# Cache attention of a sample group: four fp32 tiles of 32 columns side by side in place of high and low halves on the whole array

## The chip, the core and the metric

The kernel runs on one core of one Trainium2 chip. Its engines work from queues of their own: PE (TensorE: matmuls and transpositions), DVE (VectorE), ACT (ScalarE), POOL (GpSimd) and SP (SyncE, which here issues most DMAs). Matmul results go to PSUM, all else is held in SBUF. The metric is the device time of the core in microseconds, less is better.

## The reference, cut to what matters

One layer of a hybrid decoder in fp32, for two groups that share the weights: a prompt of 1024 tokens, and a sample group of 8 samples with 8 new tokens each (64 rows in all). The change touches the sample group's attention over its cache. Each sample has 1024 past tokens in 8 pages of 128, found through a page table; 4 heads, each with two maps of 64 (queries and keys) and values of 128:

```python
def diff_attn_block(qb, qpos_b, k, v, k_pos, rel_bias, lam):
    s = jnp.einsum('bqhcd,bkhcd->bchqk', qb, k) * (DIFF_HEAD_DIM ** -0.5)
    rel = qpos_b[:, None] - k_pos[None, :]
    bias = jnp.transpose(rel_bias[rel_bucket(rel)], (2, 0, 1))
    s = jnp.where(rel[None, None, None] >= 0, s + bias[None, None], NEG_INF)
    p = jax.nn.softmax(s, axis=-1)
    a = p[:, 0] - lam * p[:, 1]
    return jnp.einsum('bhqk,bkhe->bqhe', a, v)

k_past = cache_k[l][page_table].reshape(DB, past, N_DIFF_HEADS, 2 * DIFF_HEAD_DIM)
v_past = cache_v[l][page_table].reshape(DB, past, N_DIFF_HEADS, DIFF_V_DIM)
```

So there are 64 pages of K and 64 of V, 256 KB each. Around it: the input projection with three gate logits of width 1024, attention of the prompt, an attention over a memory, pooling, an output projection and a convolutional feed-forward block.

## The kernel before

**Number format.** Most matmuls have their operands split: `split` (L108 to 110) copies a fp32 tile, rounded, to a high half in the type fp32r (ACT, L109) and subtracts that from the tile for a low half (DVE or POOL, L110). A product is then three fp32r matmuls (high by high, high by low, low by high), each a single pass. A matmul with plain fp32 operands has two records in the trace.

**Gate logits.** Weights come in tiles `raw` (L159, two buffers, 512 KB each), are split into `hl` (five buffers; low half on POOL for these), and go to L178 (`mm_t`, prompt: `nat<-act,hl`, 24 matmuls of 512 columns for each result) and L195 (`mm_s`, sample rows: `nat<-hl,hs`). A result is copied out by `ev` (L831) and written to DRAM by `gl` (L832). There are 1344 of these L178 matmuls; nothing but the end of the layer's first half needs them, so they can fill TensorE wherever it would wait.

**What sets the order.** The program is written in stages, and when it is built a scheduler with a list of priorities puts the instructions of all stages into one fixed queue for each engine. That is how gate matmuls come to stand between those of cache attention. On the chip each queue runs strictly in order: an instruction whose operand is late holds up all behind it.

**Cache attention** (L553 to 699). Setting up: the queries are transposed, split and laid into `QS` with zeros around; the scores of the new keys against the new queries go through DRAM (`nk_d`) into `NKD`; the bias of the last 128 past positions is `dbt`. Then for each sample, twice four pages:
- `load_page` reads the page's number into a register of SP (L610) and issues the DMA (L611). The pages of K (`kr`) and V (`vr`) share three buffers of two pages each. A chain of order (`issue_after`) keeps the register read of a page behind the DMA of six pages earlier.
- The four pages are transposed head by head (L106, four transpositions of 128x128 into PSUM tiles `tp` or `av`), split into `kt`, and multiplied with `QS` by L631: 128 columns hold the high and low halves of the queries of both maps, all heads accumulate in one PSUM tile `big`.
- L651 and L652 add the halves into `E`, two samples above each other. For a pair of samples L656 subtracts the bias, L658 takes the maximum, L660 the exponential with its sum; `R` (L665) holds the reciprocal sums and the factor lambda, and L671 multiplies `E` with it in nine plain fp32 matmuls, which transposes and normalises the weights at once. They are split into `aTd`.
- The pair's V pages are split into `vh` and multiplied by L685, with 64 columns: high and low half of the weights of one sample. L688 does the new rows. The mask `hm1` keeps each head's own columns, and L695 sums the rows into `oS`.

After cache attention comes the prompt's attention (L706 to 777): per head the DMAs of `kn`, `vn`, `qT`, transpositions, scores (L741), softmax, values (L771), with gate matmuls between.

## Time and profile before

| | us |
|---|---|
| runs | 1871.69, 1870.64, 1865.92 |
| median of the runs | 1870.64 |
| profiled execution, span | 1869.5 |
| L178, the gate logits of the prompt, busy | 366.0 |
| L178, other projections, busy | 494.8 |
| L195, gate logits of the sample rows, busy | 86.4 |

The span runs from the first to the last record of the execution that was profiled. Busy times of matmuls overlap, since a matmul is counted from its start to the modelled end of its flow through the array while the next one has begun; the spacing of their starts is the price of one. The stages can be told by their first instructions: cache attention begins with the first transposition of a `kr` tile (358.5 us into the span), the prompt's attention with the first of a `kn` tile (606.7), and the projections of the two groups follow.

A row of a view of groups has the line, the engine, the operation, output and inputs by their names in the program, the shapes and the count; behind the bar the busy time in us and the mean of one in ns; behind a second bar the idle time ahead and what ended it. A row of the timeline has the start, the duration, the engine, the line and what runs. A row of the windows has the stretch and its length, the busy time of PE, PEld (weight loads), DVE, ACT and POOL in it, then that of SP, the mean granted clock of TensorE (1.00 is full), the busy share of the DMA engines and GB/s; an engine without work there may be missing.

### The profile page before, as it was taken

The page shows a single profiled execution, that of the slowest core. Times are in us where ns is not written, and L with a number is a line of the kernel's source. Part 1 is how long each engine was busy: PE and PEld are TensorE (multiplying, and loading weights), DVE is VectorE, ACT ScalarE, POOL GpSimd, SP SyncE. Part 2 cuts the span into 40 slices and gives each one's busy share as a digit, 9 for nine tenths or more (in the row PEclk, how much of TensorE's full clock was granted, in tenths as well). Part 3 has the DMA queues.
Part 4 walks back from the last instruction along what each step waited for, and adds up shares of the span by engine and source line. Part 5 has one row for each costly group of instructions (what it writes and reads, how often), then busy time and mean ns, then how long its engine had stood idle before and what let it go on. Part 6 is the DMA issues. An engine that isn't in the chain of part 4 may idle for free.

```text
span 1869.5 us, 22444 instructions
## 1 busy us (share of the span) xinstructions
PE 1807.6 (97%) x8329; PEld 1417.9 (76%) x8329; DVE 884.6 (47%) x1565; ACT 637.2 (34%) x1227; POOL 219.0 (12%) x263
## 2 busy tenths in 40 slices
PE   7999989999999999999999999999999999999997
PEld 5777866766666877777778788888888888888886
DVE  6411134255544667646733634353453453553547
ACT  5331235245444666634512432122122122221222
POOL 1113140212002342301210000000000000000000
PEclk9999999999999999999999999999999999999999
DMA  7341251365657332245561110120110110210202
GB/s 255 133 143 48 80 171 46 109 211 163 190 164 219 89 118 80 83 143 172 175 170 46 57 46 28 41 68 24 45 47 28 63 46 23 68 46 24 68 12 96
DMA packets 119457, 179.67 MB, mean 96 GB/s; under 512 B 23999, under 2 KB 61437, under 8 KB 119349
## 3 DMA queue, kind: packets, MB, share of 16 engines
q1 hardware_dynamic: 108821, 148.13, 25.9%
q0 software_dynamic: 10528, 30.12, 4.4%
q8 instruction: 65, 1.06, 0.2%
q14 instruction: 43, 0.35, 0.1%
HBM read 143.72 MB, written 34.55 MB: 95 GB/s over the span
## 4 chain that ended last, share of the span: by engine, by line
PE 78%; issue 8%; DVE 5%; DMA 4%; ACT 3%; POOL 1%; SPq 0%; POOLq 0%; ACTq 0%; DVEq 0%
PE big L178 30%; PE big L993 12%; PE nat L178 11%; PE nat L187 8%; PE nat L195 5%; PE tp L106 3%; PE av L771 2%; PE big L741 2%; DMA raw<-in_w_in 1%; PE big L631 1%; PE av L106 1%; PE big L685 1%; ACT hl L109 1%; PE av L542 1%; DMA kr<-in_cache_k 1%
## 5 line engine op out<-in xcount | busy, mean ns | idle before, releaser
L178 PE MATMUL big<-h,hl 128*128 128x512 f32 x2112 | 494.8, 394 | 0.0
L178 PEld LDWEIGHTS big<-h,hl 128*128 128x128 f32 x2112 | 395.1, 188 | 90.6 <-ACT h L109 0.3
L178 PE MATMUL nat<-act,hl 128*128 128x512 f32 x1344 | 366.0, 403 | 0.3 <-ACT ev L831 0.3
L178 PEld LDWEIGHTS nat<-act,hl 128*128 128x128 f32 x1344 | 243.7, 189 | 45.1 <-issue 2.3
L993 PE MATMUL big<-hl,ft 128*128 128x512 f32 x1056 | 241.5, 389 | 0.5 <-DVE x L995 0.5
L993 PEld LDWEIGHTS big<-hl,ft 128*128 128x128 f32 x1056 | 198.1, 188 | 42.3 <-DVE x L995 1.0
L109 ACT CAST hl<-raw 128x1024 fp32r<-128x1024 f32 x126 | 132.0, 1051 | 278.9 <-PE big L993 151.2
L110 DVE TENSOR_TENSOR hl<-raw,hl 128x1024 fp32r<-128x1024 f32 x102 | 124.4, 1222 | 162.4 <-ACT hl L109 160.7
L187 PE MATMUL nat<-hl,act 128*128 128x512 f32 x768 | 184.9, 399 | 5.9 <-DVE x1s L884 4.1
L187 PEld LDWEIGHTS nat<-hl,act 128*128 128x128 f32 x768 | 146.5, 192 | 38.1 <-issue 4.5
L995 DVE TENSOR_TENSOR x<-x,big 128x1024 f32<-128x1024 f32 x88 | 107.3, 1219 | 67.4 <-PE big L993 67.0
L958 POOL DMA_DIRECT2D out<-gu x22 | 11.9, 541 | 827.2 <-DVE gu L203 827.0
L922 DVE SCALAR_TENSOR_TENSOR t<-big,cwb,t 128x1023 f32<-128x1023 f32 x22 | 28.2, 1283 | 166.8 <-ACT t L921 166.8
L195 PE MATMUL nat<-hl,hs 128*128 128x512 f32 x336 | 86.4, 400 | 3.7 <-POOL hl L110 2.5
L195 PEld LDWEIGHTS nat<-hl,hs 128*128 128x128 f32 x336 | 63.1, 191 | 18.5 <-POOL hl L110 3.6
L949 DVE TENSOR_TENSOR t<-t,big 128x1024 f32<-128x1024 f32 x22 | 26.9, 1221 | 79.8 <-PE big L178 79.8
L110 POOL TENSOR_TENSOR hl<-raw,hl 128x1024 fp32r<-128x1024 f32 x24 | 58.3, 2434 | 43.6 <-ACT hl L109 40.3
L109 ACT CAST ft<-t 128x1024 fp32r<-128x1024 f32 x22 | 23.1, 1050 | 107.3 <-DVE t L949 107.3
L942 ACT COPY gc<-big 128x2 f32<-128x2 f32 x22 | 3.5, 160 | 162.0 <-PE big L178 162.0
L832 POOL DMA_DIRECT2D gl<-ev x48 | 26.3, 547 | 276.2 <-ACT ev L831 254.2
L110 DVE TENSOR_TENSOR vh<-vr,vh 128x512 fp32r<-128x512 f32 x64 | 46.6, 762 | 23.9 <-ACT vh L109 23.9
L752 ACT ACTIVATE E<-big,nm 128x128 f32<-128x128 f32 (+7 forms) x64 | 47.5, 742 | 22.5 <-DVE nm L749 11.7
(365 smaller groups left out, 2204.5 us busy)
## 6 DMA issues: line engine op xcount, KB each, us to landing
raw<-in_w_in SPq DMA_DIRECT2D x40, 512.0 KB
kr<-in_cache_k SPq DMA_DIRECT2D x64, 256.0 KB
vr<-in_cache_v SPq DMA_DIRECT2D x64, 256.0 KB
gl<-ev POOLq DMA_DIRECT2D x48, 256.0 KB, 2.8
raw<-in_w_ffn_gate SPq DMA_DIRECT2D x44, 256.0 KB
raw<-in_w_ffn_up SPq DMA_DIRECT2D x44, 256.0 KB
raw<-in_w_ffn_down SPq DMA_DIRECT2D x22, 512.0 KB
g<-gl SPq DMA_DIRECT2D x38, 256.0 KB
```

The lines of the kernel that those rows point to most:

```text
L106: nc.tensor.transpose(out, in_, ident[:n, :n])
L109: nc.scalar.copy(hi, src)
L110: (lo_eng or nc.vector).tensor_tensor(lo, src, hi.bitcast(F32), op=ALU.subtract)
L178: nc.tensor.matmul(out, wf(k, pw)[:, n0:n0 + P], acts[c][ph][:, k, :], start=(k == ks[0] and (pw, ph) == (0, 0)), stop=(k == ks[-1] and (p ...
L187: nc.tensor.matmul(out, acts[c][ph][:, k, o:o + P], wf(k, pw), start=(k == ks[0] and (pw, ph) == (0, 0)), stop=(k == ks[-1] and (pw, ph) = ...
L195: nc.tensor.matmul(out, stack[:, k, :], wf(k, pw), start=(k == ks[0] and pw == 0), stop=(k == ks[-1] and pw == 1))
L741: nc.tensor.matmul(S[:, k0:k0 + n], Qd[:, m, part, qs], Kst[:, m, k0:k0 + n], start=(part == 0), stop=(part == 1))
L752: nc.scalar.activation(E[:, :nk], S[:, :nk], AF.Exp, bias=nm, scale=-1.0, accum_out=ss[:, m:m + 1])
L771: nc.tensor.matmul(av[:, :P], aT[:, k * P:(k + 1) * P], vn[:, k0 + k], start=(k0 + k == 0), stop=(k0 + k == i))
L922: nc.vector.scalar_tensor_tensor(out[:, 1:], g[:, 0:T - 1], cwb[:, f, 1:2], out[:, 1:], op0=ALU.mult, op1=ALU.add)
L993: nc.tensor.matmul(pb_[:, nb], fts[k][:, ph, t * P:(t + 1) * P], wfs[nb](k, pw), start=(k == 0 and (pw, ph) == (0, 0)), stop=(k == 1 and ( ...
L995: nc.vector.tensor_tensor(x1[t], x1[t], pb_.rearrange("p c t -> p (c t)"), op=ALU.add)
```

## The change

Cache attention is laid out anew, with plain fp32 operands throughout:

- **Scores.** `QS` holds for each sample and head 32 columns of plain queries (two samples of a pair, two maps, eight rows; those of the other sample are zero). The transposed pages are copied whole into `kt`, even heads on ACT (L638), odd heads on DVE (L636). When all four heads are there, L644 runs four matmuls, one for each head, each with 32 columns of weights on its own quarter of the array's columns (`tile_position`), written one behind the other. Both samples of a pair accumulate in the same PSUM rows.
- **Weights.** `E` has the rows by head, sample, map, and 1152 columns; L652 and L653 copy the scores from PSUM on ACT, L654 subtracts the bias while copying the last 128 columns. The mask between samples for the new rows lies in `NKD`, which is filled with -1e30 and gets eight small DMAs instead of two. L667 and L670 form the transposed weights as before, but `aT` stays plain, with four buffers.
- **Values.** They are done for four samples at once, after the weights of two pairs: for each page number `kb`, L696 runs four matmuls side by side, one for each sample, on the pages of V as they are; the ninth group is the new rows (`vsf`). `hm1` and the selection matmul (now L704) run once for four samples.
- **Buffers.** The pages of K and V share five tiles of two pages instead of three.

```diff
-        qsT = dc.tile([P, 2, NH, TS], F32R, name="qsT")
+        QS = dc.tile([P, DB, NH, 32], F32, name="QS")
+        nc.gpsimd.memset(QS, 0.0)
...
-        nc.gpsimd.dma_start(bass.AP(nk_d.tensor, nk_d.offset, [[TS, TS], [8 * 512, 2 * NH], [1, TS]]),
-                            nks.rearrange("p (c t) -> p c t", t=TS))
-        NKD = dc.tile([P, DB // 2, DS], F32, name="NKD")
-        for par in range(2):
-            nc.gpsimd.dma_start(NKD[par * TS:par * TS + TS],
...
+        for c in range(2):
+            nc.gpsimd.dma_start(bass.AP(nk_d.tensor, nk_d.offset + c * 4096, [[TS, TS], [8192, NH], [1, TS]]),
+                                nks[:, c * 256:(c + 1) * 256].rearrange("p (h t) -> p h t", t=TS))
+        NKD = dc.tile([P, DB // 2, 2, DS], F32, name="NKD")
+        nc.gpsimd.memset(NKD, -1e30)
+        for h in range(NH):
+            for s2 in range(2):
+                r0 = h * 32 + s2 * 16
+                nc.gpsimd.dma_start(NKD[r0:r0 + 16, :, s2],
...
-        for b in range(DB):
...
-                    k_ = dc.tile([P, 2, 512], F32, tag="kr", bufs=3, name=f"kr{uid()}")
...
+        def scores(b, ch, Sb):
+            kr = []
+            for i in range(2):
+                k_ = dc.tile([P, 2, 512], F32, tag="kr", bufs=5, name=f"kr{uid()}")
+                for u in range(2):
+                    load_page(k_[:, u], cache_k, b * NPG + ch * 4 + i * 2 + u)
+                kr.append(k_)
+            kt = dc.tile([P, NH, 512], F32, tag="kt", bufs=2, name=f"kt{uid()}")
+            for h in range(NH):
+                pt = tpb()
+                for i in range(4):
+                    tr(pt[:, i * P:(i + 1) * P], kr[i // 2][:, i % 2, h * P:(h + 1) * P])
+                if h % 2:
+                    nc.vector.tensor_copy(kt[:, h], pt)
+                else:
+                    nc.scalar.copy(kt[:, h], pt)
+            first = None
+            for h in range(NH - 1, -1, -1):
+                with ExitStack() as es:
+                    if first is not None:
+                        es.enter_context(tc.issue_after(first.ins))
+                    m = nc.tensor.matmul(Sb[h * 32:(h + 1) * 32, ch], QS[:, b, h], kt[:, h], start=(b % 2 == 0),
+                                         stop=(b % 2 == 1), tile_position=(0, h * 32))
+                first = first or m
+
+        def weights(p, Sb):
+            E = dc.tile([P, 1152], F32, tag="E", bufs=2, name=f"Ed{p}")
+            nc.gpsimd.memset(E[:, 1024:1152], -1e30)
+            nc.vector.tensor_copy(E[:, 1024 + 16 * p:1040 + 16 * p], NKD[:, p].rearrange("p s t -> p (s t)"))
+            nc.scalar.copy(E[:, 0:512], Sb[:, 0])
+            nc.scalar.copy(E[:, 512:896], Sb[:, 1, 0:384])
+            nc.vector.tensor_tensor(E[:, 896:1024], Sb[:, 1, 384:512], dbt, op=ALU.subtract)
...
+            aT = dc.tile([P, 9, TS], F32, tag="aT", bufs=4, name=f"aTd{p}")
...
+            for kb in range(8):
+                nc.tensor.matmul(pa[:, kb * TS:(kb + 1) * TS], E[:, kb * P:(kb + 1) * P], R, start=True, stop=True)
+            nc.scalar.copy(aT[:, 0:8].rearrange("p k r -> p (k r)"), pa)
...
+        for g in range(2):
+            aTs = []
+            for p in (2 * g, 2 * g + 1):
+                Sb = big()
+                for b in (2 * p, 2 * p + 1):
+                    for ch in range(2):
+                        scores(b, ch, Sb)
+                aTs.append(weights(p, Sb))
+            X = big()[:, 0]
             for kb in range(9):
...
+                        vr = dc.tile([P, 2, 512], F32, tag="kr", bufs=5, name=f"vr{uid()}")
+                        for u in range(2):
+                            load_page(vr[:, u], cache_v, (4 * g + 2 * i + u) * NPG + kb)
...
+                        m = nc.tensor.matmul(X[bl * 32:(bl + 1) * 32],
+                                             aTs[bl // 2][:, kb, (bl % 2) * 32:(bl % 2) * 32 + 32],
+                                             vrs[bl // 2][:, bl % 2] if kb < 8 else vsf,
+                                             start=(kb == 0), stop=(kb == 8), tile_position=(0, bl * 32))
...
+            nc.vector.tensor_tensor(om, X, hm1, op=ALU.mult)
             pn = tpb()
...
+            nc.tensor.matmul(pn[:32], selb, om, start=True, stop=True)
+            nc.vector.tensor_copy(oS[g * 32:(g + 1) * 32], pn[:32])
```

The scheduler orders the queues anew. Three places are shown; a row there is the line, the operation, output and inputs with the numbers of their buffers, the shape of the output, and how many in a row.

**TensorE, the end of the first pair's scores.** Before, gate matmuls (L178, on the weights `hl`) stand ahead of the matmuls L671 that form the weights `tp` out of `Ed` and `R`, and behind them:

```order
L178 MATMUL nat_7266<-act_145,hl_7180 128x512 x2
L178 MATMUL nat_7266<-act_146,hl_7180 128x512
L178 MATMUL nat_7266<-act_145,hl_7180 128x512
L178 MATMUL nat_7266<-act_145,hl_7185 128x512
L178 MATMUL nat_7266<-act_146,hl_7185 128x512
L178 MATMUL nat_7266<-act_145,hl_7185 128x512
L671 MATMUL tp_2853<-R_2851,Ed_2666 128x64 x8
L671 MATMUL big_2854<-R_2851,Ed_2666 64x64
L178 MATMUL nat_7266<-act_145,hl_7185 128x512
```

Now, the transpositions of the last pages, the score group L644, the weights and the next sample's transpositions follow each other:

```order
L106 MATMUL av_2781<-ident,kr_2720 128x128 x2
L106 MATMUL av_2781<-ident,kr_2741 128x128 x2
L644 MATMUL big_2506<-kt_2762,QS 32x512 x4
L667 MATMUL tp_2807<-R_2804,Ed_2791 128x64 x8
L670 MATMUL av_2817<-R_2804,Ed_2791 128x64
L106 MATMUL av_2870<-ident,kr_2821 128x128
L106 MATMUL tp_2864<-ident,kr_2821 128x128 x2
```

The 27 gate matmuls that stood between the scores and the weights of the pair are no longer there.

**TensorE, the last values of the stage.** Before, the value matmuls (L685, on the split pages `vh`) alternate with gate matmuls:

```order
L685 MATMUL big_4744<-vh_4942,aTd_4754 64x512
L178 MATMUL nat_7770<-act_147,hl_7707 128x512
L685 MATMUL big_4744<-vh_4942,aTd_4754 64x512
L178 MATMUL nat_7770<-act_147,hl_7712 128x512
L685 MATMUL big_4744<-vh_4968,aTd_4754 64x512
L178 MATMUL nat_7770<-act_148,hl_7712 128x512
```

Now the value groups of samples 4 to 7 (L696) stand alone, and the next gate matmuls come behind them, on weights `hl` that are loaded later:

```order
L696 MATMUL big_4140<-vr_4484,aTd_4126 32x512 x2
L696 MATMUL big_4140<-vr_4463,aTd_3812 32x512 x2
L696 MATMUL big_4140<-vsf,aTd_4126 32x512 x2
L696 MATMUL big_4140<-vsf,aTd_3812 32x512 x2
L195 MATMUL nat_6955<-hl_6937,hs 128x512 x4
L704 MATMUL av_4515<-omd_4513,selb 32x512
L195 MATMUL nat_6955<-hl_6942,hs 128x512 x4
```

Counted over the whole stage (from the first transposition of `kr` to the first of `kn`), 453 matmuls of L178 and 36 of L195 stood in it before, 199 and 20 do now; the other 270 stand further back.

**SP, the end of the pages.** Before, the last page of V (L611) is followed by the DMAs of the prompt's attention, `NB` and `kn`; the weights of the gates (`raw`, L159) stood further ahead, twelve of them among the pages:

```order
L610 TENSOR_LOAD pgt
L610 ISA x2
L611 ISA
L611 DMA vr_4978<-in_cache_v 128x512
L706 DMA NB<-nb_d 128x256 x4
L710 DMA kn_5027<-k_d 128x8x128
```

Now four of the gates' weight tiles stand behind the last page, ahead of `NB` and `kn`, and one among the pages:

```order
L621 DMA vr_4484<-in_cache_v 128x512
L159 DMA raw_6935<-in_w_in 128x2x512
L159 DMA raw_6940<-in_w_in 128x2x512
L159 DMA raw_6945<-in_w_in 128x2x512
L159 DMA raw_6950<-in_w_in 128x2x512
L712 DMA NB<-nb_d 128x256 x4
L716 DMA kn_4528<-k_d 128x8x128
```

So the matmul L195 that follows the last value group works on the first of these tiles.

More of the change, by code (lines that the diff above doesn't have):

```diff
@@ L690, in hybrid_step @@
-            om = dc.tile([P, 512], F32, tag="om", bufs=2, name=f"omd{b}")
-            for bb in range(2):
-                nc.vector.tensor_tensor(om[bb * TS:(bb + 1) * TS], X[:TS, bb], hm1[:TS], op=ALU.mult)
-            pn = tpb()
-            o0 = 48 - 8 * (b - 1)
-            nc.tensor.matmul(pn[:TS], selb[:, o0:o0 + TS], om, start=True, stop=True)
-            if b == 1:
-                nc.vector.tensor_copy(oS, pn[:TS])
-            else:
-                nc.vector.tensor_tensor(oS, oS, pn[:TS], op=ALU.add)
+            for kb in range(8):
+                nc.tensor.matmul(pa[:, kb * TS:(kb + 1) * TS], E[:, kb * P:(kb + 1) * P], R, start=True, stop=True)
@@ new lines, in weights @@
+            nc.scalar.copy(aT[:, 0:8].rearrange("p k r -> p (k r)"), pa)
+            pn = tpb()
+            nc.tensor.matmul(pn[:, :TS], E[:, 1024:1152], R, start=True, stop=True)
+            nc.vector.tensor_copy(aT[:, 8], pn[:, :TS])
+            return aT
+        for g in range(2):
[7 more added lines that the diff above has]
+            X = big()[:, 0]
+            for kb in range(9):
+                vrs = []
+                if kb < 8:
+                    for i in range(2):
+                        vr = dc.tile([P, 2, 512], F32, tag="kr", bufs=5, name=f"vr{uid()}")
+                        for u in range(2):
+                            load_page(vr[:, u], cache_v, (4 * g + 2 * i + u) * NPG + kb)
+                        vrs.append(vr)
+                first = None
+                for bl in range(3, -1, -1):
+                    with ExitStack() as es:
+                        if first is not None:
+                            es.enter_context(tc.issue_after(first.ins))
+                        m = nc.tensor.matmul(X[bl * 32:(bl + 1) * 32],
+                                             aTs[bl // 2][:, kb, (bl % 2) * 32:(bl % 2) * 32 + 32],
+                                             vrs[bl // 2][:, bl % 2] if kb < 8 else vsf,
+                                             start=(kb == 0), stop=(kb == 8), tile_position=(0, bl * 32))
+                    first = first or m
+            om = dc.tile([P, 512], F32, tag="om", bufs=2, name=f"omd{g}")
+            nc.vector.tensor_tensor(om, X, hm1, op=ALU.mult)
+            pn = tpb()
+            nc.tensor.matmul(pn[:32], selb, om, start=True, stop=True)
+            nc.vector.tensor_copy(oS[g * 32:(g + 1) * 32], pn[:32])
```

119 lines of the change are left out of this document (31 added, 88 removed).

## The prediction

> **What bounds the kernel now.** I read the page from the top: the span, the engines' shares, the slices, then the chain that ended last.
>
> ```profile
> span 1869.5 us, 22444 instructions
> PE 1807.6 (97%) x8329; PEld 1417.9 (76%) x8329; DVE 884.6 (47%) x1565; ACT 637.2 (34%) x1227; POOL 219.0 (12%) x263
> PEclk9999999999999999999999999999999999999999
> PE 78%; issue 8%; DVE 5%; DMA 4%; ACT 3%; POOL 1%; SPq 0%; POOLq 0%; ACTq 0%; DVEq 0%
> ```
>
> TensorE is busy for 97% of the span, at full clock. So a microsecond of matmul taken out counts, as long as something else is ready to run in its place. Next come the stages: the windows from the first transposition of a K page (358.5) to the first of the prompt's keys (606.7), and the two stages after it.
>
> ```profile
> 358.50:606.70 248.20, 236.47 (x1098) 163.07 (x1097) 124.47 (x207) 111.37 (x184) 35.55 (x33) 0.99 0.59 184
> 606.70:786.00 179.30, 173.23 (x991) 139.24 (x990) 117.97 (x305) 117.97 (x309) 60.79 (x68) 1.00 0.28 85
> 786.00:860.00 74.00, 69.94 (x319) 53.42 (x318) 40.19 (x130) 33.54 (x70) 9.41 (x12) 1.00 0.52 167
> ```
>
> The cache stage takes 248.2 us, PE busy 236.5. What keeps it busy is told by the groups of that window, the largest of which is not cache attention at all but gate logits put between:
>
> ```profile
> L178 PE MATMUL nat<-act,hl 128*128 128x512 f32 x454 | 132.4, 404 | 0.0
> L631 PE MATMUL big<-kt,QS 128*128 128x512 f32 x128 | 51.6, 447 | 3.5 <-ACT kt L109 2.5 <-DVE kt L110 0.9
> L685 PE MATMUL big<-vh,aTd 128*64 128x512 f32 x128 | 44.0, 413 | 4.2 <-DVE vh L110 4.1
> L106 PE MATMUL tp<-ident,kr 128*128 128x128 f32 x128 | 26.9, 278 | 3.6 <-DMA kr<-in_cache_k 3.6
> L106 PE MATMUL av<-ident,kr 128*128 128x128 f32 x128 | 23.7, 273 | 0.0
> L195 PE MATMUL nat<-hl,hs 128*128 128x512 f32 x36 | 11.2, 430 | 0.0
> L695 PE MATMUL av<-omd,selb 128*64 128x512 f32 x8 | 4.3, 618 | 0.0
> ```
>
> These busy times overlap, so I price a matmul by its spacing in a dense run, from the timeline:
>
> ```profile
> 512.26 6.28 PE L178 MATMUL nat<-act,hl 128*128 128x512 f32 x27
> 371.26 0.60 PE L106 MATMUL tp<-ident,kr 128*128 128x128 f32 x4
> 518.87 1.97 PE L671 MATMUL tp<-R,Ed 128*128 128x64 f32 x16 [0.33 <-DVE R L665]
> 276.39 1.09 PE L508 MATMUL big<-mv,PTs 128*32 128x256 f32 x16
> 277.41 0.66 PE L106 MATMUL tp<-ident,mk 128*128 128x128 f32 x4
> ```
>
> ```profile
> 302.81 0.86 PE big L523 x2
> ```
>
> A split matmul of 512 columns is 6.28/27 = 0.23 us. A transposition is (0.60 - 0.27)/3 = 0.11, 0.44 for four. L671 has 16 records for 8 matmuls of the program: plain fp32 is two passes, about 2.0 us for a pair's nine. **The best row for the change is L508**: plain fp32 on 32 columns, four tiles, in the attention over the memory. Sixteen records of 256 columns last from 276.39 until the next start at 277.41, 1.02 us. On the whole array two plain passes of 512 columns (L523, from the chain in order of time) take 0.86, so sixteen passes of 256 one after another would take 3.4. Four tiles do run side by side here, each four passes of 256 deep; the changed kernel issues two passes of 512 deep in each: **1.02 us for a group of four**.
>
> **What goes and what comes, on PE.** Before: 453 + 36 gate matmuls x 0.23 = 112.5; 256 transpositions 27.9; L671 8.0; 256 score and value matmuls of L631 and L685, and 16 of the new rows' values, x 0.23 = 62.6; L695, eight passes of 512 at half speed, 3.5. Sum 214.5 of 248.2, so the stage holds **33.7 us of waiting**; much of it hides in busy time (L631 and L685 are busy 95.6 us for 256 x 0.23 = 58.9). After: 16 score groups and 18 value groups x 1.02 = 34.7; L704 has half of L695's passes, 1.7; transpositions and weights stay, 35.9. That is 72.3 against 102.0: **29.7 us less PE work**. DVE and ACT lose the splits of K and V; DVE is busy for 124 of 248 us, so this saves nothing by itself.
>
> But the order shows the second effect. The changed stage holds only 199 + 20 gate matmuls: **270 are moved behind it, 270 x 0.23 = 62.1 us**, into the stages after, which the windows above show already full (173 of 179, 70 of 74). The stage must get shorter by more than 62.1 us before anything is won. Its PE work is now 219 x 0.23 + 72.3 = 122.7. So what decides is how much it will wait.
>
> **What paces the changed stage: the pages on SP's queue.** 128 pages of 256 KB, each a register load, checks and a DMA.
>
> ```profile
> L611 SPq DMA_DIRECT2D kr<-in_cache_k x6: 337/338/387, 348.4 to 354.7; - x6
> L610 SPq TENSOR_LOAD <-pgt x5: 262/263/282, 367.6 to 369.9; - x5
> L611 SPq DMA_DIRECT2D kr<-in_cache_k x4: 332/333/347, 365.6 to 367.2; - x4
> 390.00:397.00 7.00, 6.99 (x33) 5.62 (x32) 5.21 (x10) 2.97 (x5) 0.54 (x1) 1.00 0.97 329
> SPq L611 <- PE av L106: 43.3, 16, 6.9
> SPq L611 <- DVE vh L110: 30.9, 18, 8.0
> ```
>
> The first six pages start 1.25 us apart. Apart from that, a register load takes (369.9 - 367.6)/4 = 0.58 and an issue (367.2 - 365.6)/3 = 0.53: 1.11. I take 1.15, nearer to the second, whose loads are not the slow first ones; 4.6 us for four pages. The DMA engines themselves carried 329 GB/s, 0.8 us a page, so they are not the limit. Before, SP waited 43 + 31 us for a free buffer (three tiles, six pages); now ten pages fit. I count 2.4 us from issue to landing, the distance that the first group had.
>
> The rest of the walk needs the softmax chain of a pair and the weight splits:
>
> ```profile
> 512.46 1.01 ACT L651 COPY Ed<-big 64x1024 f32<-64x1024 f32 x1 [0.33 <-PE big L631]
> 513.50 1.23 DVE L652 TENSOR_TENSOR Ed<-Ed,big 64x1024 f32<-64x1024 f32 x1 [0.50 <-ACT Ed L651]
> 515.09 1.29 DVE L658 TENSOR_REDUCE nm<-Ed 128x1 f32<-128x1088 f32 x1
> 516.75 1.21 ACT L660 ACTIVATE Ed<-Ed,nm 128x1088 f32<-128x1088 f32 x1 [3.28 <-DVE nm L658]
> 520.88 0.59 ACT L109 CAST aTd<-tp 128x512 fp32r<-128x512 f32 x1 [2.36 <-PE tp L671]
> L110 POOL TENSOR_TENSOR hl<-raw,hl 128x1024 fp32r<-128x1024 f32 x10 | 23.9, 2400 | 31.8 <-ACT hl L109 28.6 <-issue 3.2
> L109 ACT CAST hl<-raw 128x1024 fp32r<-128x1024 f32 x10 | 10.4, 1044 | 1.4 <-DMA raw<-in_w_in 0.7 <-PE nat L178 0.6
> ```
>
> From 512.46 to L671's start at 518.87 it is 6.4 us; L652 goes (1.26 with its gap), the subtraction of the bias moves beside the copies (0.3), 1152 columns instead of 1088 add 0.15: **5.0 us**, and 0.8 until the transposed weights are out of PSUM. A score group is 16 x 0.11 + 1.02 = 2.8 us of PE; its four copies (0.59 on ACT, 0.69 on DVE, two PSUM buffers) pace it at about 2.9. Now stage by stage, in the new order:
>
> - Samples 0 to 3, scores (no gates between after the first 18): the first four groups find their pages and end at 375.5. PE waits out the softmax, 380.5, and forms the weights, 382.5. Two groups have pages in the ten slots, two wait for slots: 397.5. Softmax and weights again, 405. PE works 30 of these 46.5 us.
> - Values 0 to 3: two groups at once (407), two that wait for pages (415), four with 18 gates each (4.1 + 1.0): 436; the new rows and L704, 438.
> - Scores 4 and 5, 13 gates a group, 5.8 x 4: 461; 21 gates cover the softmax: 466, weights 468. Scores 6 and 7, 20 gates in all: 484; 13 gates cover 3.0 of 5.0; weights and copy: 492.
> - Values 4 to 7, no gate between them: ten pages are there, 22 come at 1.15 = 25.3 us: 518, the last group and the new rows 520. PE has 9 us of work in these 28.
> - The next gates' weights stand in SP's queue behind the last page: landing at 519, four tiles through ACT (1.04) and POOL (2.4 each), the last two loaded only when a buffer is free again, 2.9 us each: 533, where the prompt's first keys follow.
>
> One more price stands in the windows around 375:
>
> ```profile
> 374.50:377.00 2.50, 0.55 (x4) 0.20 (x2) 1.73 (x5) 1.95 (x2) 0.46 (x1) 1.00 0.92 333
> 377.00:380.60 3.60, 3.38 (x10) 2.75 (x10) 1.29 (x2) 1.07 (x2) 1.89 (x1) 0.53 0.74 203
> ```
>
> After PE had hardly run for 2.5 us, its granted clock was 0.53 for the next 3.6, which costs some 1.7 us. Two uncovered softmaxes and the wait at the end are such pauses: 5 us, end at **538**.
> [...]
>
> **The sum.** Stage 538 - 358.5 = 179.5 instead of 248.2: 68.7 us less. Moved gates: 62.1 more. Net -6.6, span 1863. In other words 29.7 us of work are saved and the waiting grows from 33.7 to 56.8. The median of the runs shown (1870.64) is 1.1 above this span, so **1864**.
>
> The edits ahead of the stage cost nothing as long as they end before the first K copy:
>
> ```profile
> L595 POOL DMA_DIRECT2D NKD<-nk_d x2: 621/634/647, 343.6 to 344.2; - x2
> 362.55 0.59 ACT L109 CAST kt<-tp 128x512 fp32r<-128x512 f32 x1 [7.27 <-PE tp L106]
> ```
>
> Ten small DMAs on POOL where there were three, 0.63 us each and from 343.6 on as these, are done around 352, ten us ahead. If POOL were late, DVE's first K copies would stand behind the masks that wait for them. Bound: 0 to 4 us.
>
> The 0.16 us between L508's 1.02 and 0.86 is what a group pays for starting and draining; it is in the sum 34 times, 5.4 us, and less where two groups follow each other directly.
> [...]
>
> **Rivals.**
>
> *The queue never stands still* (chance 0.20). If slots free early enough that SP issues all 128 pages without waiting, 128 x 1.15 = 147 us after 348.7, the last page lands at 498 and everything after it comes 20 us sooner, with a part of the clock price gone: 1841. For it: ten slots instead of six. Against: SP cannot run ahead while PE sits in a softmax with all ten full.
>
> *The clock stays down: slower* (0.28). In samples 0 to 3 PE works 30 of 46.5 us in bits. If the clock is halved there throughout, PE needs up to 60, 14 us beyond the walk, and the weights' matmuls and first gates at the end 3 more; less the 5 counted, +12 to +15: 1878. It decides once pauses as in 374.5:377.0 recur within each few microseconds; between 363 and 374, with waits of 0.2 to 0.6 us, the clock stayed up, which speaks against it. The turning point for slower than before is a stage of over 186 us.
>
> *The tiles do not run side by side* (0.05). Eight passes of 512 columns one after another, 8 x 0.43 = 3.5 us, 2.5 more a group. Where PE waits for pages anyway some is hidden: about 63 us, 1927. L508 speaks plainly against it.
>
> **How the numbers follow.** Forecast, 1857 to 1871: 0.43. The rest, 0.04, is something not listed. About 0.3%, 5.6 us, is what a measurement of this kernel can tell from no change: faster means below 1865.0, slower above 1876.2. Faster: 0.25 of the forecast's and all of the first rival's 0.20: 0.45. Slower: 0.20 of the clock's, 0.05 of the tiles' and 0.04: 0.29. Within: 0.18 and 0.08: 0.26. The range for 8 in 10 takes in the first rival and the clock's, without the tiles: 1838 to 1886.
>
> **What would show it.** Score and value groups of 1.0 us in the rows of L644 and L696, 8 records each, starts within some tens of ns of each other; SP's page DMAs 1.15 us apart with few waits; PE idle ahead of L667 by some 5 us twice and between the last eight value groups by 3 us each; the first `kn` transposition at 533 to 538; the last gate matmul, at 844 before, no more than a few us earlier. Wrong would be a group of 3.5 us, a stage end before 520 or after 545, or gates that find room in the prompt's attention and so cost less than 62 us.

## The result and the profile after

| | kernel before | changed kernel |
|---|---|---|
| median of the runs, us | 1870.55 (1865.92 to 1871.69) | 1891.01 (1886.55 to 1895.7) |
| ratio to before, 95% interval | | 1.0115 (1.0094 to 1.0137) |
| span of the profiled execution, us | 1869.5 | 1893.9 |

The change made the kernel 20 us slower; 1864 was forecast, with 1838 to 1886 as the range. The execution profiled after the change is the slowest of its four (1895.7), so differences between the two traces come out some 4 us larger than those of the medians.

The page of the changed kernel: span, engines, granted clock in 40 slices.

```profile
span 1893.9 us, 22046 instructions
PE 1791.8 (95%) x8325; PEld 1396.6 (74%) x8325; DVE 806.1 (43%) x1414; ACT 580.2 (31%) x1127; POOL 222.3 (12%) x272
PEclk9999999979879999999999999999999999999999
```

TensorE has 15.8 us less busy time than before and yet the span is 24.4 us longer. The clock, at 90% or more in every slice before, falls below that in slices 9, 11 and 12 (47 us each), in the cache stage. The instructions of L106 and of the projection behind the gates (L195 on `bs_stack`) give the edges of the stages (count, shortest/median/longest in ns, first and last start in us):

```profile
L106 PE MATMUL tp<-ident,kr x128: 270/273/476, 359.8 to 497.6; 128*128 128x128 f32 x128
L106 PE MATMUL tp<-ident,kn x32: 272/273/327, 555.6 to 690.5; 128*128 128x128 f32 x32
L195 PE MATMUL nat<-hl,bs_stack x32: 389/389/499, 866.6 to 927.8; 128*128 128x512 f32 x32
```

The same instructions before:

```profile
L106 PE MATMUL tp<-ident,kr x128: 270/272/476, 358.7 to 566.9; 128*128 128x128 f32 x128
L106 PE MATMUL tp<-ident,kn x32: 272/273/301, 607.0 to 744.6; 128*128 128x128 f32 x32
L195 PE MATMUL nat<-hl,bs_stack x32: 388/389/526, 844.5 to 904.4; 128*128 128x512 f32 x32
```

So the cache stage went from 248.2 to 195.8 us, 52 less, and the stretch from the first `kn` to the end of the gates from 237.5 (844.5 - 607.0) to 311.0, 73.5 more. The windows of the changed kernel: the stage, its first softmax with the weights behind it, the second, the last values, the stretch after the stage, and the time from the first softmax to the next pair's first score group.

```profile
359.80:555.60 195.80, 152.63 (x824) 88.12 (x823) 36.30 (x64) 41.21 (x67) 17.10 (x16) 0.83 0.64 197
380.00:389.00 9.00, 4.07 (x18) 3.91 (x18) 2.29 (x6) 2.67 (x5) 0.00 (x0) 0.55 0.38 112
407.10:416.20 9.10, 4.07 (x18) 3.91 (x18) 2.22 (x5) 2.71 (x5) 0.00 (x0) 0.56 0.60 178
507.40:540.40 33.00, 15.77 (x72) 2.15 (x72) 0.22 (x1) 0.56 (x2) 0.00 (x0) 0.55 0.65 207
555.60:866.40 310.80, 294.81 (x1509) 234.21 (x1510) 158.22 (x422) 159.05 (x385) 85.22 (x95) 0.98 0.32 101
380.90:394.60 13.70, 9.43 (x42) 7.93 (x46) 3.96 (x9) 3.55 (x6) 0.20 (x1) 0.50 0.26 72
```

PE stands idle for 43 of the stage's 195.8 us, and when it works it is often at half clock: behind the first softmax that lasts for 13.7 us. What it waits for, by the view of waits of that window (line, releaser, total us, times, longest):

```profile
PE big L696 <- DMA vr<-in_cache_v: 19.5, 8, 3.5
PE tp L667 <- DVE R L663: 10.1, 2, 5.0
PE tp L106 <- ACT kt L638: 3.1, 7, 0.6
```

Pages of V, and the two softmaxes with nothing between. The score groups of the first pair, with one of the copies between them and the transpositions behind it; the weights behind the softmax; the first two value groups; and value groups near the end, from the timeline:

```profile
365.69 1.06 PE L644 MATMUL big<-kt,QS 128*32 128x512 f32 x8
370.01 1.07 PE L644 MATMUL big<-kt,QS 128*32 128x512 f32 x8
371.85 0.59 ACT L638 COPY kt<-tp 128x512 f32<-128x512 f32 x1 [2.44 <-PE tp L106]
372.49 0.65 PE L106 MATMUL tp<-ident,kr 128*128 128x128 f32 x4 [0.61 <-ACT kt L638]
374.37 1.06 PE L644 MATMUL big<-kt,QS 128*32 128x512 f32 x8
378.72 1.07 PE L644 MATMUL big<-kt,QS 128*32 128x512 f32 x8 [0.78 <-DVE kt L636]
384.82 3.64 PE L667 MATMUL tp<-R,Ed 128*128 128x64 f32 x16 [5.03 <-DVE R L663]
...
416.44 3.64 PE L696 MATMUL big<-vr,aTd 128*32 128x512 f32 x16 [0.25 <-ACT aTd L668]
...
517.69 1.94 PE L696 MATMUL big<-vr,aTd 128*32 128x512 f32 x8 [3.46 <-DMA vr<-in_cache_v]
522.35 1.94 PE L696 MATMUL big<-vr,aTd 128*32 128x512 f32 x8 [2.73 <-DMA vr<-in_cache_v]
526.92 1.93 PE L696 MATMUL big<-vr,aTd 128*32 128x512 f32 x8 [2.64 <-DMA vr<-in_cache_v]
531.32 1.93 PE L696 MATMUL big<-vr,aTd 128*32 128x512 f32 x8 [2.47 <-DMA vr<-in_cache_v]
```

A group of four tiles takes 1.06 us at full clock and 1.94 at half, so the tiles do run side by side. But score groups come 4.3 us apart, L667 takes 3.64 instead of 1.97 after a 5.03 us pause, and value groups come 4.6 us apart, the time of four pages. The score groups do not wait for pages there. The transpositions that feed the next copies stand behind the group in PE's queue: ACT waits 2.44 us for them, and then PE waits 0.61 us for ACT's copy.

### The profile page after: what moved, and what is told of

The parts are those of the page before. It is cut to its first block, busy times and chain, and to the rows that moved or that the text cites. A ratio compares the mean times of both kernels' runs of the same rounds, so it can differ in the third digit from the quotient of the medians.

```text
span 1893.9 us, 22046 instructions
## 1 busy us (share of the span) xinstructions
PE 1791.8 (95%) x8325; PEld 1396.6 (74%) x8325; DVE 806.1 (43%) x1414; ACT 580.2 (31%) x1127; POOL 222.3 (12%) x272
## 3 DMA queue, kind: packets, MB, share of 16 engines
q8 instruction: 65, 1.06, 0.2%
## 4 chain that ended last, share of the span: by engine, by line
PE 78%; DVE 5%; DMA 5%; issue 5%; ACT 3%; SPq 3%; POOL 1%; ACTq 0%; POOLq 0%; DVEq 0%
PE big L178 29%; PE nat L178 12%; PE big L999 12%; PE nat L187 8%; PE nat L195 4%; PE tp L106 3%; PE av L777 2%; PE av L106 2%; PE big L747 2%; DMA raw<-in_w_in 2%; ACT hl L109 1%; PE av L542 1%; PE big L644 1%; SPq L620 1%; POOL hl L110 1%
## 5 line engine op out<-in xcount | busy, mean ns | idle before, releaser
L178 PE MATMUL big<-h,hl 128*128 128x512 f32 x2112 | 494.8, 394 | 0.0
L178 PEld LDWEIGHTS big<-h,hl 128*128 128x128 f32 x2112 | 395.1, 188 | 90.5 <-ACT h L109 0.3
L178 PE MATMUL nat<-act,hl 128*128 128x512 f32 x1344 | 350.7, 404 | 0.0
L178 PEld LDWEIGHTS nat<-act,hl 128*128 128x128 f32 x1344 | 248.2, 191 | 51.9 <-issue 6.7
L195 PE MATMUL nat<-hl,hs 128*128 128x512 f32 x336 | 91.5, 413 | 7.3 <-POOL hl L110 3.7
L195 PEld LDWEIGHTS nat<-hl,hs 128*128 128x128 f32 x336 | 64.1, 196 | 29.3 <-POOL hl L110 6.1
L837 ACT COPY ev<-nat 128x512 f32<-128x512 f32 x48 | 28.1, 585 | 113.5 <-PE nat L178 113.4
L747 PE MATMUL big<-Kst,Qd 128*128 128x512 f32 (+3 forms) x192 | 53.6, 374 | 1.0 <-ACT E L758 0.7
L178 PE MATMUL big<-ob,hl 128*128 128x512 f32 x192 | 51.1, 401 | 2.9 <-DVE g L871 2.3
```

Of the source, the lines that this page charges most:

```text
L178: nc.tensor.matmul(out, wf(k, pw)[:, n0:n0 + P], acts[c][ph][:, k, :], start=(k == ks[0] and (pw, ph) == (0, 0)), stop=(k == ks[-1] and (p ...
L195: nc.tensor.matmul(out, stack[:, k, :], wf(k, pw), start=(k == ks[0] and pw == 0), stop=(k == ks[-1] and pw == 1))
L747: nc.tensor.matmul(S[:, k0:k0 + n], Qd[:, m, part, qs], Kst[:, m, k0:k0 + n], start=(part == 0), stop=(part == 1))
L837: nc.scalar.copy(ev, pt)
```

## The experiments

The theory after this reading is called *missing gates*: the cache stage takes its time by pages, copies and softmaxes almost whatever TensorE does meanwhile; what counts is how many gate matmuls stand in it, since each one that doesn't is paid in full behind it. In the tables, gate matmuls are those of L178 and L195 that the order puts between the first transposition of `kr` and the first of `kn`; the stage is the time between these two. Each ratio is to runs of the kernel before that were made beside that run; their medians lie between 1868.9 and 1870.6.

| run | gate matmuls in the stage | stage, us | median, us | ratio to before (95%) |
|---|---|---|---|---|
| before | 489 | 248.2 | 1870.55 | |
| changed | 219 | 195.8 | 1891.01 | 1.0115 (1.0094 to 1.0137) |
| e1_gates_pool | 438 | 194.2 | 1836.29 | 0.9834 (0.9805 to 0.9862) |
| e2_before_gates_pool | 502 | 247.8 | 1878.26 | 1.0047 (1.003 to 1.0063) |
| e3_fill | 241 | 200.4 | 1890.58 | 1.0117 (1.0095 to 1.0138) |
| e4_three_buffers | 437 | 228.0 | 1866.66 | 0.9989 (0.9974 to 1.0004) |
| e5_scores_late | 41 | 186.6 | 1927.74 | 1.0306 (1.0289 to 1.0324) |
| e6_values_only | 394 | 215.7 | 1866.2 | 0.9987 (0.9978 to 0.9997) |
| e7_gates_act_dve | 441 | 192.3 | 1821.99 | 0.9744 (0.9728 to 0.9761) |
| e8_gates_pool_scores_late | 438 | 196.2 | 1840.86 | 0.9834 (0.981 to 0.9857) |
| e9_before_act_dve | 524 | 247.6 | 1851.51 | 0.9893 (0.9866 to 0.9921) |
| e10_values_only_act_dve | 474 | 218.2 | 1834.49 | 0.9796 (0.9766 to 0.9826) |
| e11_three_buffers_act_dve | 519 | 219.9 | 1828.78 | 0.9789 (0.9755 to 0.9822) |
| e12_fill_few_gates | 41 | 186.5 | 1925.98 | 1.0294 (1.0271 to 1.0318) |

### The gates' weights on another queue

```diff
-    def load_w(srcs, lo_eng=None, rp=None):
+    def load_w(srcs, lo_eng=None, rp=None, q=None):
...
-                nc.sync.dma_start(raw[:, :, c0:c1], src.rearrange("(k p) n -> p k n", p=P))
+                (q or nc.sync).dma_start(raw[:, :, c0:c1], src.rearrange("(k p) n -> p k n", p=P))
...
-                wf = load_w(cols(w_in, 2048 + g * D + nb * 512), nc.gpsimd)
+                wf = load_w(cols(w_in, 2048 + g * D + nb * 512), nc.gpsimd, q=nc.gpsimd)
```

> The changed kernel with one edit: the DMAs of the gates' weights (raw) are issued by POOL instead of SP, where they stood behind the pages; the scheduler then puts 406 prompt and 32 sample gate matmuls into the cache stage instead of 199 and 20. Theory 'missing gates' (the stage lost the work that fills its waits, and the clock falls in the pauses): stage PE work 122.7 + 219 x 0.23 = 173 us with few pauses, so the stage ends no later than 565 instead of 555.6 while some 60 us leave the stages behind it: 1830 to 1850 us. Rival 'pages and softmax pace the stage whatever stands between': the gates lengthen the stage by what they take, 1885 to 1893 us.

Measured 1836.3, in the theory's range. The window of its stage, and what PE waits for there:

```profile
363.20:557.40 194.20, 187.03 (x1043) 119.40 (x1042) 36.98 (x65) 49.71 (x79) 38.38 (x40) 0.98 0.70 220
```

```profile
PE nat L195 <- POOL hl L110: 3.8, 2, 1.9
PE nat L195 <- ACT hl L109: 2.0, 2, 1.3
PE big L696 <- DMA vr<-in_cache_v: 0.8, 3, 0.3
```

219 more gate matmuls stand in a stage that is 1.6 us shorter, though by their spacing of 0.23 us they are 50 us of work; that the time falls as they come in bears the theory out. How much of it is their cover and how much the higher clock that they bring, this run doesn't part. The 19.5 us of waiting for V pages are 0.8, the waits for the softmaxes are gone, the clock is 0.98 instead of 0.83. The same cache attention code is here 2.8% faster than in the changed kernel. SP was also freed of the weights' DMAs by this edit, but the stage's length, which would show faster pages, hardly moved.

> The kernel before with the same edit (gates' weights issued by POOL; 470 and 32 gate matmuls in the stage instead of 453 and 36). Theory 'missing gates': its stage was filled already, so 1865 to 1875. Rival 'the other queue is worth something by itself': 1840 to 1860.

Measured 1878.3, slower than the kernel before, and 3 us above what was expected. So POOL's queue is worth nothing to a stage that is filled already. The stage of this run begins at 366.9 instead of 358.7. POOL forms the low halves and now issues the loads too, one behind the other, which fits but was not tried apart.

### Three buffers instead of five

The edit is `bufs=3` for both tiles of the tag `kr`.

> The changed kernel with three page buffers as before instead of five; SP then waits for buffers, and the scheduler places 12 weight loads among the pages, 401 and 36 gate matmuls in the stage. Theory 'missing gates': faster than the changed kernel by 15 to 40 us, 1850 to 1875, though SP can load fewer pages ahead. Rival 'the pages pace': fewer pages ahead make it slower than the changed kernel, 1895 to 1915.

Measured 1866.7: faster than the changed kernel by 24 us, although the stage is 32 us longer (228.0). SP waits for buffers, the scheduler puts twelve weight tiles between the pages, and the gates are back. With the two extra buffers of the change SP's queue was full of pages, and the weights came behind them.

### Still fewer gates

The edit keeps a score group back until the next half's transpositions are issued:

```diff
-            first = None
-            for h in range(NH - 1, -1, -1):
+            flush()
+            pend.append((b, ch, Sb, kt))
+
+        pend = []
+
+        def flush():
+            if not pend:
+                return
+            b, ch, Sb, kt = pend.pop()
+            first = None
+            for h in range(NH - 1, -1, -1):
...
+                flush()
                 aTs.append(weights(p, Sb))
```

> The changed kernel with each score group written one half later, behind the next half's transpositions; by this the scheduler leaves only 37 prompt and 4 sample gate matmuls in the cache stage (199 and 20 in the changed kernel). Theory 'missing gates': 178 more matmuls go behind the stage, 41 us, and the stage can shrink only as far as pages and softmaxes let it, by 6 to 20: 1912 to 1926 us, slower still. Its score groups should come closer together where pages are there: 2.9 to 3.4 us instead of 4.33, if it was the group standing between the transpositions that spread them. Rival 'the spread score groups cost the time': 1870 to 1885.

Measured 1927.7, a little above the range of the theory and far from the rival. With 178 gate matmuls fewer the stage gets only 9.2 us shorter. From 41 to 219 to 438 gate matmuls (this run, the changed kernel, the first) the time falls by 36.7 and 54.7 us: 0.21 and 0.25 us for each. The second expectation missed: the score groups did not come closer.

```profile
369.54 1.06 PE L653 MATMUL big<-kt,QS 128*32 128x512 f32 x8
374.01 1.07 PE L653 MATMUL big<-kt,QS 128*32 128x512 f32 x8
378.51 1.07 PE L653 MATMUL big<-kt,QS 128*32 128x512 f32 x8
```

They are 4.5 us apart, since the scheduler put the group between half-done transpositions of the next half instead of behind them. So the cycle is the one of the changed kernel: in this trace, too, ACT waits 2.59 us across the group (to 375.63), until the rest of the transpositions is done, and PE then 0.61 us for ACT's copy.

> Gates' weights on POOL's queue and score groups one half later; 406 and 32 gate matmuls in the stage as without the second edit. Theory 'missing gates': with gates between them the score groups wait for nothing, so nothing is won: 1833 to 1840 us. Rival 'the spread score groups cost time by themselves': 1815 to 1828.

Measured 1840.9, just above the theory's range; the ratio is 0.9834 as without the second edit: with gates between them, the place of the score groups is worth nothing.

### Is it the clock?

Matmuls whose result nobody reads fill the pauses: `nc.tensor.matmul(pd, ident, kt[:, 0])`, in plain fp32, put behind the scores ahead of L667, and between the last value groups.

> The changed kernel with matmuls that compute nothing needed (plain fp32, 128x512, 0.43 us each at full clock) in the pauses: 10 in each of the first two softmaxes, 4 in the last, 5 ahead of each of the last seven value groups; 221 and 20 gate matmuls stay in the stage, nearly as now. Theory 'the clock': TensorE stays at full clock, which gives back about 15 us of the stage (windows 380:416 5.9, 416:454 4.2, after the last page 5): 1873 to 1880. Rival 'the clock costs nothing, the pages pace': 1888 to 1895.

Measured 1890.6, no change. The clock did stay up, as the window of the stage shows:

```profile
358.50:558.90 200.40, 190.33 (x965) 106.65 (x964) 39.19 (x64) 42.48 (x69) 20.55 (x19) 0.99 0.65 203
```

```profile
379.78 7.46 PE L657 MATMUL tp<-kt,ident 128*128 128x512 f32 x17
387.07 1.89 PE L681 MATMUL av<-R,Ed 128*128 128x64 f32 x16
```

But the dose was wrong. A pass of plain fp32 took 7.46/17 = 0.44 us and each matmul has two, so ten of them last 8.8 us and not 4.3: the weights (L681 here) start 3.6 us after they could, though they then take 1.89 instead of 3.64. The last value groups are held up too: they come 5.5 us apart, the time of a group and its filling, instead of 4.6. What the clock gave went into overlong filling, and the run doesn't tell.

> The changed kernel with fewer idle matmuls in the pauses than in the first such run (they took 0.87 us each there, not 0.43): 5 in each of the first two softmaxes, 2 in the last, 3 ahead of each of the last seven value groups. The scheduler now leaves 37 and 4 gate matmuls in the stage, exactly as many as in the run with the scores one half later (1927.7 us, whose stage held 126 us of PE work at a mean clock well below 1 and 66 us idle), so it is compared with that one. Theory 'the clock is paid for on the path where PE is late, and hidden where pages are': some 8 to 20 us less, 1908 to 1920. Rival 'hidden behind pages everywhere': 1924 to 1930.

Measured 1926.0, in the rival's range. The windows of the stages of the two runs with 41 gate matmuls, this one first:

```profile
356.30:542.80 186.50, 140.23 (x713) 69.98 (x712) 35.70 (x63) 33.63 (x56) 6.19 (x6) 0.84 0.64 188
```

```profile
363.30:549.90 186.60, 120.83 (x647) 61.51 (x645) 35.70 (x63) 33.58 (x56) 6.22 (x6) 0.73 0.62 188
```

The clock rose from 0.73 to 0.84 and the stage stayed as long. The two runs also differ in the place of the score groups, and the filling takes time on PE, so this is no clean test of the clock. That it costs nothing where PE waits for pages is argued from the changed kernel's rows: from 509.8 to 533.4 SP issues pages 1.12 us apart, and PE stands waiting 2.5 to 3.5 us for them ahead of each group. Neither run shows what a full clock without overlong filling would give the changed kernel; it stays open between 0 and the 15 us that were expected.

### One half of the change

In this run the scores are as before the change, the values as after it.

> Only the values are changed (four samples side by side, plain fp32, five page buffers); scores and softmax as before the change. 374 and 20 gate matmuls in the stage. Theory 'missing gates': 95 matmuls fewer than before in the stage, about 22 us, against some 15 us less work for values: 1868 to 1882, nearer to the kernel before than to the changed one. Rival 'the values of four samples at a time are what is slow (33 us of page pace at the end)': 1885 or more.

Measured 1866.2, slightly below the range; 394 gate matmuls kept their place here. The side-by-side values are not slow by themselves. This run has five page buffers as well, so the buffers alone don't drive the gates out; it takes them together with the new scores.

### The cost of the gates' halves, and what the change is worth with gates in place

To the first edit, ACT's queue instead of POOL's, and the low halves on DVE:

```diff
-                wf = load_w(cols(w_in, 2048 + g * D + nb * 512), nc.gpsimd)
+                wf = load_w(cols(w_in, 2048 + g * D + nb * 512), nc.vector, q=nc.scalar)
```

> As the run with the gates' weights on POOL's queue, but issued by ACT, and with the low half of the gates' weights formed by DVE (1.2 us) instead of POOL (2.4 us); 409 and 32 gate matmuls in the stage. That run's TensorE waited 5.0 us for the high and 4.9 us for the low halves: 1826 to 1834 us if those waits go; 1836 to 1842 if ACT's queue holds the DMAs up.

Measured 1822.0, below both ranges: 2.6% faster than the kernel before, the fastest of this study. The edit changes two things at once, and which of them brings the 14 us against POOL's queue was not tried. Its stage:

```profile
354.40:546.60 192.20, 184.50 (x1045) 118.51 (x1046) 47.62 (x76) 49.59 (x79) 11.34 (x22) 1.00 0.74 236
```

PE waits 7.7 us in it at full clock, while it does the work of 441 gate matmuls besides cache attention. The same edit on the other kernels:

> The kernel before with the gates' weights issued by ACT and their low half on DVE (492 and 32 gate matmuls in the stage). Theory 'missing gates': this kernel lacked few gates, so the edit is worth little to it, 1855 to 1872, and the 47 us by which the changed kernel with the same edit beats the kernel before are mostly the change's own 29.7 us of work plus waiting. Rival 'the edit alone is worth what was won': 1825 to 1840.

> Only the values changed, with the gates' weights issued by ACT and their low half on DVE; 442 and 32 gate matmuls in the stage. If with gates in place the change is worth its saved work, the values' part (about 15 of 29.7 us) shows: midway between the two kernels with the same queue, 1838 to 1850. If the values cost as much as they save: 1855 to 1870.

> The changed kernel with three page buffers, the gates' weights issued by ACT and their low half on DVE; 487 and 32 gate matmuls in the stage, about as many as in the kernel before with this edit. Theory 'missing gates': with them there the two extra page buffers matter little, 1816 to 1830. Rival 'pages need the five buffers': 1840 or more.

Measured 1851.5, 1834.5 and 1828.8; the first two are 3.5 us below their ranges, so the edit is worth more to the kernel before than thought, but not what the rival asked. On the kernel before the edit alone brings 20 us. With the same edit on both, the changed kernel against the kernel before is 0.9744/0.9893 = 0.985: 28 us, beside the 29.7 us of PE work by which the prediction priced the change. The stage of the kernel before with this edit:

```profile
355.40:603.00 247.60, 240.15 (x1132) 167.62 (x1133) 130.51 (x220) 110.19 (x183) 12.86 (x25) 1.00 0.58 186
```

PE waits 7.4 us in it, as little as the 7.7 above, and the clock is full in both. The changed kernel's stage is 55.3 us shorter and holds 83 gate matmuls fewer, 19 us; so cache attention takes some 36 us less of PE, an estimate from these figures, of which 28 are left in the whole. Of the 28 the values bring 18 (0.9893 - 0.9796 of 1870) and the scores the rest. Three buffers with gates in place cost 7 us by the medians (1828.8 against 1822.0), but the intervals just touch, so it may be less or nothing.

## Why the prediction was wrong

**What held.** Groups of four tiles: 1.02 us forecast, and 0.99 measured from the start of a score group to the next matmul (365.69 to 366.68); a value group with another right behind it took 0.88 (450.09 to 450.97), the less that was forecast for such groups, though what the difference is spent on no run shows. Softmax without cover: 5.0 forecast, 5.03 and 5.04 measured. The page cadence of 1.15:

```profile
L621 SPq DMA_DIRECT2D vr<-in_cache_v x22: 332/333/342, 509.8 to 533.4; - x22
```

The last 22 pages went out (533.4 - 509.8)/21 = 1.12 us apart. That the change saves PE work of about the size that was priced, 29.7 us, shows once the gates are in place (28 us in the whole). And the second effect, 270 gate matmuls moved out of the stage, was named as what decides.

**What failed is the size of the two terms that were to cancel, the stage above all.** The sum said: stage 68.7 us less, moved gates 62.1 more, so 6.6 faster. Measured, the stage is 52.4 less and the gates 73.5 more:

- *The stage, 195.8 instead of 179.5: 16.3 short.* Step by step, measured against the walk: samples 0 to 3 up to the second pair's weights 56.4 us (359.8 to 416.2) instead of 46.5; their values 37.8 (to 454.0) instead of 33; scores and weights of samples 4 to 7 53.4 (to 507.4) instead of 54; their values 33.0 (to 540.4) instead of 28; the weights behind the last page 15.2 instead of 13. That is 21.3 too little, against the 5 that the sum added for the clock.
  - The step that failed first is the score group. The walk took 2.9 us, paced by its four copies as if these ran on beside the group's matmuls. They don't: by the rows of L644 it is (378.72 - 365.69)/3 = 4.3 in the first pair, where the copies wait for transpositions that stand behind the group, and 4.0 in the second. Some 6 of the 9.9 us that samples 0 to 3 took longer are this.
  - The clock was named but priced too low. L667 ran 1.7 us longer in each uncovered softmax, just what the sum had for a pause. But the prediction took that price from a stretch of 3.6 us at half clock, and here it lasted 13.7 us: the first two value groups behind the second softmax took 3.64 us together instead of 2.0, and at the end the last group and the new rows 3.6 instead of 2.0.
  - The pages of the last values go out from 509.8 on, 2.4 us after that step began, where the walk had SP issue them from its start. What the rest of these 21.3 us is was not followed.
- *The moved gates, 73.5 instead of 62.1: 11.4 short.* The prediction priced them by the spacing of a dense run and gave them no waiting. By the window 555.6:866.4 PE is idle for 16.0 us there; before, it was 6.1 + 3.8 = 9.9 in the windows of 606.7 to 844.5, the second of which is the row below. Three pauses of PE between 748 and 765, of 1.8, 1.5 and 4.0 us, are more than these 6 us; what stands there is told in the last section. The other 5 are matmuls at a lower clock: 0.98 over the window, where both windows before have 1.00.

```profile
786.00:844.50 58.50, 54.70 (x254) 42.13 (x253) 29.98 (x115) 26.95 (x59) 7.22 (x10) 1.00 0.49 158
```

- The start of the stage (1.1 later) and what lies behind the gates (2.3 longer in this execution) make the rest: 16.3 + 11.4 + 1.1 + 2.3 = 31.1, between the forecast span of 1862.9 and 1893.9.

**The rivals.** The clock that stays down was the nearest, with its sign and 1878, and its condition came true in part: in samples 0 to 3 the clock was at half for 13.7 us behind the first softmax and again behind the second, but not throughout, and the score groups of the first pair ran at full clock (1.06 us each, and 1.00 over 359.8 to 380.0). Its turning point, a stage of over 186 us, was passed too. But that it is the clock that costs the time is not shown: keeping it up with empty matmuls won nothing, with fillings that were too long to tell. *The queue never stands still* did not come: SP waited for buffers for 36.7 us in all.

```profile
SPq L621 <- PE tp L106: 13.9, 9, 6.6
SPq L621 <- PE big L696: 11.6, 5, 5.1
SPq L621 <- PE av L106: 11.2, 4, 7.1
```

That is the difference between 128 x 1.15 = 147 and the 184 us from the first page's DMA to the last.

The mistake behind the sizes is one of view. The prediction walked along the stage to find how short it becomes with few gates, and the runs say that it hardly becomes shorter: 186.5 us with 41 gate matmuls, 192.3 with 441. A stage with such a floor should be asked how much other work fits in it for nothing, and the answer here was 400 gate matmuls, some 93 us of work by their spacing, for 6 us, had the weights come in time (the two runs differ in other things too).

## What to carry to other kernels

When a change makes a stage lighter, look first at what other work used to fill its waits and whether that work's loads still reach it: here two more buffers, with the lighter scores, kept one queue busy with pages, the filler's weights ended up behind them, and a saving of 28 us became a loss of 20. In this kernel it paid to put the loads of filler work on a queue that the stage they are to fill doesn't use. Price work that is moved out of a stage in full, with waits, and compare the length of the stage with and without it before counting on it to shrink.

## What the runs showed of the hardware that was not expected

*Beside POOL's subtractions, DVE instructions with two inputs in SBUF took 2.3 us instead of 0.15, and up to 2.48 instead of 0.34.* Behind the stage the changed kernel has POOL's low halves of the moved gates beside DVE's work for the projections. First DVE, then POOL, from the timeline:

```profile
759.73 0.17 DVE L118 RECIPROCAL rsy<-rst 128x4 f32<-128x4 f32 x1
759.82 2.32 DVE L122 TENSOR_TENSOR rsy<-rsy,rst 128x4 f32<-128x4 f32 x2
762.06 2.31 DVE L119 TENSOR_TENSOR rst<-rsy 128x4 f32<-128x4 f32 x1
764.29 0.86 DVE L800 SCALAR_TENSOR_TENSOR g<-g,rsy,gsub 128x128 f32<-128x128 f32 x3
```

```profile
759.69 4.66 POOL L110 TENSOR_TENSOR hl<-raw,hl 128x1024 fp32r<-128x1024 f32 x2 [0.18 <-ACT hl L109]
```

Beside each of POOL's two instructions (2.3 us) one of DVE's with two inputs took as long, 2.25 us in L122 and 2.31 in L119, where others of the same lines take 0.15; L118, with one input, took 0.17 beside POOL. At that place PE stands still for 4.04 us. The view names no releaser for it; the transposition behind the pause reads the `g` that L800 writes at the end of these rows. Two shorter pauses of PE just ahead, 1.8 and 1.5 us, wait for DVE beside another two of POOL's instructions (747.84 to 752.56). The five microseconds behind the long pause run at half clock:

```profile
765.00:770.00 5.00, 5.00 (x17) 3.86 (x17) 4.25 (x16) 0.89 (x2) 0.00 (x0) 0.50 0.22 51
```

The longest L800 of each kernel, 2.48 and 0.35 us, agrees, the changed one first and then the one with the low halves on DVE:

```profile
L800 DVE SCALAR_TENSOR_TENSOR g<-g,rsy,gsub x32: 335/343/2482, 746.1 to 775.3; 128x128 f32<-128x128 f32 x32
```

```profile
L800 DVE SCALAR_TENSOR_TENSOR g<-g,rsy,gsub x32: 335/347/352, 734.8 to 759.1; 128x128 f32<-128x128 f32 x32
```

Before the change (L794 there, 801.7 to 819.1) its longest was 0.35 us; POOL formed no low halves in that time. Why the two then take equally long no run shows. This is one of the prices of moved work that no count of matmuls shows.

*The granted clock fell to half soon after a pause of 2.03 us, and stayed there through pauses of 2.5 to 3.5 us.* Two windows in the last values of the changed kernel:

```profile
511.00:514.00 3.00, 0.97 (x12) 0.16 (x8) 0.00 (x0) 0.00 (x0) 0.00 (x0) 1.00 0.81 262
514.10:540.40 26.30, 11.51 (x52) 1.40 (x48) 0.00 (x0) 0.20 (x1) 0.00 (x0) 0.50 0.71 228
```

In the first PE waits 2.03 us and then works on one group, still at full clock; from 514 on it works 1.9 us and waits 2.5 to 3.5 us in turn, and the granted clock is 0.50 throughout. The pause of 2.03 us is not the only one near: PE waited 2.13 us ahead of 505.17, and from 509 to 511, busy throughout, it had 0.60. In the row that the prediction quoted, 2.5 us with 0.55 of work in it were followed by 3.6 us at 0.53.
